# Which engine waits for the last store: GpSimd in place of SyncE at the end of a batched matmul

## The chip, the cores and the metric

One core of one Trainium2 chip. The metric is the device time of one execution in microseconds (us), median of several runs. The kernel before takes 125.6 us.

## The reference

```python
batch, m, k, n = 16, 512, 512, 512          # a: [16, 512, 512], b: [16, 512, 512], float32
def reference(a, b):
    return np.matmul(a, b.transpose(0, 2, 1)).astype(np.float32)
```

## The kernel before

The kernel loads `a` and `b` in 16 transfers of 2 MB, casts to bf16, transposes and multiplies on TensorE, evicts on ScalarE, and stores 16 results of 1 MB. Semaphores are handled by hand inside two critical sections. GpSimd (POOL in the profile) issues the stores 0 to 7, SyncE (SP) the stores 8 to 15, and each store has its own semaphore `s_st[n]`.

```python
    with tc.tile_critical(no_gpsimd_drain=True):
        # ... buffers, semaphores, loads ...
        STORES = "SSSSOSOSOSSOOOOOO"        # GpSimd: S issues a store, O hands a buffer back
        LATE = {11: (8, 9), 13: (10, 11), 15: (12, 13)}     # SyncE's stores, by load

        def landed(n):
            return s_st[n], 16

        def store(n):
            engine = nc.gpsimd if n < STORES.count("S") else nc.sync
            engine.wait_ge(s_out, n + 1)
            engine.dma_start(
                out[n].rearrange("(p j) n -> p j n", j=J), ob[:, n % NO]
            ).then_inc(s_st[n], 16)
        # ... SyncE: loads and its stores, then:
        store(batch - 2)
        store(batch - 1)
        for n in range(batch - NO, batch - 1):
            nc.sync.wait_ge(*landed(n))
        # ... VectorE, ScalarE, TensorE ...

    with tc.tile_critical(no_gpsimd_drain=True):
        nc.sync.wait_ge(*landed(batch - 1))
```

Leaving a section is a handshake: the engine that heads the section gives a signal, the other engines of the section answer, each with a drain (with `no_gpsimd_drain`, GpSimd with a plain NOP). After the second section the program closes by itself: every engine drains, GpSimd gathers their signals and releases them, clears the semaphores, and does this barrier once more. GpSimd's own drain stands just ahead of its gathering.

## Time and profile before

| | before |
|---|---|
| time, median | 125.6 us |
| span, first to last instruction | 123.9 us |
| the last store lands | 122.52 us |
| from there to the end of the span | 1.41 us |
| GpSimd's first closing DRAIN | 120.40 to 121.11 us, 714 ns |

The times of single instructions below are read from the trace, to the nanosecond. "Landing" is the 16th and last increment of the last store's semaphore. The quoted views give starts to 0.1 us. In them a row such as `L287 POOLq DRAIN  x3: 34/130/714, 123.3 to 124.7; - x3` names the source line, the engine (q: handled by its sequencer), the operation, how many there were, the shortest, median and longest duration in ns, and the start of the first and the last. L287 is the end of the program, to which the closing barrier is booked; L260 is the `with` of the second section.

### The profile page before, as it was taken

How to read it: one execution, taken by the hardware profiler on the slowest of the kernel's cores; microseconds unless marked ns; L12 is line 12 of the kernel's file. 1: busy time of each engine (PE TensorE's matmuls, PEld its weight loads, DVE VectorE, ACT ScalarE, POOL GpSimd, SP SyncE). 2: the span in 40 equal slices, each digit the busy share in tenths (PEclk: the TensorE clock that was granted, in tenths of full speed). 3: DMA queues.
4: the chain of work that ended last, by engine and by line, in shares of the span. 5: the costliest groups of instructions: out<-in, count | busy, mean ns of one | idle time of the engine just before them, and what ended most of it. 6: DMA issues, size and time to landing. Idle time of an engine off the chain costs nothing. (4 is left out here: it accounts for less than half of the span.)

```text
span 123.9 us, 2364 instructions
## 1 busy us (share of the span) xinstructions
PE 91.9 (74%) x768; PEld 56.9 (46%) x768; DVE 68.5 (55%) x96; ACT 68.0 (55%) x130; POOL 5.5 (4%) x14
## 2 busy tenths in 40 slices
PE   0005099998999899999989998996699919995000
PEld 0005096457447644764575467444554518441000
DVE  0006596938891897489478658914957068400000
ACT  4002415669558937876595579534956069655000
POOL 2000000000000070001010120000000000000000
PEclk9999999999999999999999999999999986999955
DMA  4999999999999998999999999999999999999980
GB/s 95 397 423 434 428 428 428 423 434 423 428 434 439 439 423 360 439 439 412 436 420 431 450 420 420 431 431 450 410 436 428 410 434 423 423 431 426 434 368 8
DMA packets 4608, 50.33 MB, mean 406 GB/s; under 512 B 512, under 2 KB 512, under 8 KB 512
## 3 DMA queue, kind: packets, MB, share of 16 engines
q1 hardware_dynamic: 3456, 41.94, 80.3%
q0 software_dynamic: 1152, 8.39, 16.0%
HBM read 33.55 MB, written 16.78 MB: 406 GB/s over the span
## 5 line engine op out<-in xcount | busy, mean ns | idle before, releaser
L247 PE MATMUL ps<-tb,ta 128*128 128x512 bf16 x256 | 57.8, 379 | 0.5
L205 ACT COPY ob<-ps 128x512 f32 x64 | 34.4, 589 | 31.1 <-PE ps L247 21.5
L187 ACT COPY ta<-tp 128x512 bf16<-128x512 bf16 x64 | 32.8, 610 | 13.8 <-PE tp L228 13.8
L247 PEld LDWEIGHTS ps<-tb,ta 128*128 128x128 bf16 x256 | 24.1, 97 | 30.6 <-issue 4.0
L228 PE MATMUL tp<-ident,ha 128*128 128x128 bf16 x256 | 20.1, 234 | 14.1 <-PEq L133 14.1
L228 PEld LDWEIGHTS tp<-ident,ha 128*128 128x128 bf16 x256 | 17.0, 105 | 17.9 <-issue 16.0
L168 DVE COPY tb<-tp 128x1024 bf16<-128x1024 bf16 x32 | 21.2, 684 | 4.8 <-DVEq L133 4.8
L228 PE MATMUL tp<-ident,hb 128*128 128x128 bf16 x256 | 18.8, 232 | 6.7 <-PEq L133 6.7
L228 PEld LDWEIGHTS tp<-ident,hb 128*128 128x128 bf16 x256 | 16.6, 105 | 7.2 <-issue 7.2
L152 DVE CAST hb<-ld 128x1024 bf16 x8 | 5.5, 689 | 12.6 <-DVEq L133 12.5
L163 DVE COPY ha<-wa 128x2048 bf16<-128x2048 bf16 x8 | 5.5, 690 | 11.1 <-DVEq L133 11.1
L152 DVE CAST ha<-ld 128x1024 bf16 x8 | 5.6, 705 | 9.8 <-DVEq L133 9.8
L158 DVE CAST wa<-ld 128x2048 bf16 x8 | 9.8, 1220 | 0.0
L158 DVE CAST wb<-ld 128x2048 bf16 x8 | 9.8, 1219 | 0.0
L103 POOL DMA_DIRECT2D out_dram<-ob x8 | 4.8, 607 | 65.5 <-DMA ld<-in_b_dram 41.5
L155 DVE CAST ha<-ld 128x1024 bf16 x8 | 5.6, 700 | 0.0
L167 DVE COPY hb<-wb 128x2048 bf16<-128x2048 bf16 x8 | 5.5, 685 | 0.2
L155 DVE CAST hb<-ld 128x1024 bf16 x8 | 5.5, 686 | 0.0
L178 ACT ACT_TABLE_LOAD x1 | 1.3, 1283 | 1.1 <-SPq L43 1.1
L79 POOL TENSOR_SCALAR_AFFINE_SELECT ident<-ident 128x128 bf16<-128x128 bf16 x1 | 0.3, 284 | 0.2 <-POOL ident L77 0.2
L77 POOL MEMSET ident<- 128x128 bf16 x1 | 0.2, 205 | 0.5 <-SPq L43 0.5
L178 ACT COPY one<-const-float32-1.0 128x1 f32<-128x1 f32 x1 | 0.2, 192 | 0.0
(4 smaller groups left out, 0.4 us busy)
## 6 DMA issues: line engine op xcount, KB each, us to landing
ld<-in_a_dram SPq DMA_DIRECT2D x8, 2048.0 KB, 28.1
ld<-in_b_dram SPq DMA_DIRECT2D x8, 2048.0 KB, 30.4
out_dram<-ob POOLq DMA_DIRECT2D x8, 1024.0 KB, 29.2
out_dram<-ob SPq DMA_DIRECT2D x8, 1024.0 KB, 19.7
```

The costliest lines, as they stand in the source:

```text
L103: engine.dma_start(out[n].rearrange("(p j) n -> p j n", j=J), ob[:, n % NO]).then_inc(s_st[n], 16)
L152: nc.vector.tensor_copy(out=h[:, :J, :], in_=src[:, :J, :HK]).then_inc(s_cd, 1)
L155: nc.vector.tensor_copy(out=h[:, J:, :], in_=src[:, J:, :HK]).then_inc(s_c, 1)
L158: nc.vector.tensor_copy(out=w[:], in_=src[:, :, HK:]).then_inc(s_w, 1)
L163: nc.vector.tensor_copy(out=ha[:], in_=wa[:]).then_inc(s_ca, 1)
L167: nc.vector.tensor_copy(out=hb[:], in_=wb[:]).then_inc(s_cb, 1)
L168: nc.vector.tensor_copy(out=tb[:, ko, :], in_=tp[:, 2 + ko % 2].rearrange("k j p -> k (j p)"),).then_inc(s_eb, 1)
L178: nc.scalar.copy(out=one[:], in_=nc.const_aps.tensor(1.0, (P, 1), f32))
L187: c = nc.scalar.copy(out=ta[:, ko, e * J * P:(e + 1) * J * P].rearrange("k (j p h) -> k j p h", j=J, h=2), in_=tp[:, ko % 2, :, e * HP:(e ...
L205: c = nc.scalar.copy(out=dst[:, j, :].rearrange("m (p j) -> m p j", j=2 * J), in_=ps[:, j, :].rearrange("m (j p) -> m p j", j=2 * J),)
L228: t = nc.tensor.transpose(tp[:, 2 * x + g, j, :], h[:, j, g * P:(g + 1) * P], ident[:])
L247: t = nc.tensor.matmul(ps[:, j, :], ta[:, ko, (e * J + j) * P:(e * J + j + 1) * P], tb[:, ko, :].rearrange("k (j p) -> k j p", j=2 * J)[:, ...
```

## The change

The wait for the last store, the only instruction of the second section, goes to another engine. The intent is to take the last wait off SyncE.

```diff
     with tc.tile_critical(no_gpsimd_drain=True):
-        nc.sync.wait_ge(*landed(batch - 1))
+        nc.gpsimd.wait_ge(*landed(batch - 1))
```

## The prediction

> **What bounds the kernel now.** The kernel before takes 125.58 us (125.56 to 125.77); its profiled execution took 125.75 us, of which the span from first to last instruction is 123.9 us. I call the remaining 1.85 us launch overhead and take it as unchanged, because no instruction of the kernel lies in it. I read the whole page first, to see what is full:
>
> ```profile
> PE   0005099998999899999989998996699919995000
> POOL 2000000000000070001010120000000000000000
> DMA  4999999999999998999999999999999999999980
> DMA packets 4608, 50.33 MB, mean 406 GB/s; under 512 B 512, under 2 KB 512, under 8 KB 512
> ```
>
> The DMA row stands at 9 from the second slice to the last but two: the 50.33 MB of loads and stores set the time, and the matrix engine stops three slices (some 9 us) before the end. GpSimd (POOL) is nearly empty. The change touches no load, store or computation, so the body of the kernel, up to the last store, should be the same to the noise. All that can move is the tail, so I then read windows of the end (columns: window, length, busy us of each engine with instruction counts, granted clock, DMA share, GB/s):
>
> ```profile
> core 0: us, PE busy (x) PEld busy (x) DVE busy (x) ACT busy (x) POOL busy (x), PEclk, DMA share, GB/s
> ...
> 118.00:120.00 2.00, 0.00 (x0) 0.00 (x0) 0.00 (x0) 0.00 (x0) 0.00 (x0) 0.58 1.00 422
> 120.00:121.00 1.00, 0.00 (x0) 0.00 (x0) 0.00 (x0) 0.00 (x0) 0.00 (x0) 0.50 0.49 205
> 121.00:122.50 1.50, 0.00 (x0) 0.00 (x0) 0.00 (x0) 0.00 (x0) 0.00 (x0) 0.50 0.04 16
> 122.50:123.90 1.40, 0.00 (x0) 0.00 (x0) 0.00 (x0) 0.00 (x0) 0.00 (x0) 0.50 0.00 0
> ```
>
> Data moves at full rate until 120, trickles until 122.5, and then there are 1.4 us without data or computation. The last store is issued at 113.95 and takes 8.6 us to land (the view of DMA issues), so it lands at 122.52. The wait for it is the last line here (SyncE's own waits; total us, times, longest):
>
> ```profile
> SPq L119 <- DMA out_dram<-ob: 5.7, 3, 2.4
> ...
> SPq L287 <- DMA out_dram<-ob: 1.7, 1, 1.7
> ```
>
> L119 is the three earlier waits for stores inside the first section, L287 (the line that closes the program) the one that the change moves. The sequencer instructions of L287, by engine:
>
> ```profile
> L287 SPq EVENT_SEMAPHORE  x5: 17/28/1689, 120.7 to 123.9; - x5
> L287 POOLq EVENT_SEMAPHORE  x4: 17/17/17, 123.0 to 123.8; - x4
> L287 POOLq DRAIN  x3: 34/129/714, 120.4 to 123.7; - x3
> L287 SPq DRAIN  x3: 7/7/7, 122.9 to 123.2; - x3
> ...
> L287 POOLq EVENT_SEMAPHORE_RANGE_CLEAR  x1: 287/287/287, 123.4 to 123.4; - x1
> ```
>
> (duration ns min/median/max, start of the first and the last.) The 1689 ns is SyncE waiting for the last store, 120.86 to 122.55. The 714 ns is GpSimd's own first DRAIN of the closing barrier, started at 120.40 and done at 121.11: at present it is finished 1.4 us before the last store lands, so it is free. That is the fact on which my prediction rests.
>
> **What the Trainium skill says.** Perfetto Trace Analysis, section Sequencer-only Instruction: the reported time of such an instruction is its execution alone, not its semaphore wait. The single waits here agree (GpSimd's gathering wait shows 17 ns although GpSimd stood there for 1.9 us); the two-semaphore wait for the last store differs, it shows the whole 1689 ns. PSUM — Partial Sum Buffer, section Engine vs sequencer instructions: a drain waits for the engine to go fully idle. Here SyncE, ScalarE and VectorE drain in 7 to 10 ns and GpSimd in 34 to 714 ns, the longest one 15 us after GpSimd's previous instruction, so idleness alone doesn't explain its cost. GPSIMD Engine Reference, section Instruction dispatch: a GpSimd instruction passes its sequencer and then a dispatcher on eight cores; I take this as a possible reason for a dear drain, which no number here proves. DMA: Bandwidth & Descriptors, section Why a DMA increments its semaphore by 16 and not by 1: only the full 16 means landed. The trace agrees: the last store's 15th increment comes at 121.28, the 16th at 122.52. Which engine waits doesn't move that.
>
> **The change, part by part.** Removed: SyncE's wait for the last store, and with it SyncE's part in the second section. Added: the same wait on GpSimd, preceded on GpSimd by the entry waits of the section, which on SyncE are two of 28 ns plus gaps, over by 120.86. They stay under the 1.7 us for which the store is still in flight: cost nothing.
> Moved: what follows the landing. Before, by the starts in the trace: landing 122.524; SyncE's wait ends 122.546; its branch 122.584 (33 ns); the leaving handshake of the section 122.739, 122.824 and 122.897; two SyncE drains 122.941 and 123.005; GpSimd's gathering wait 123.036. That is 0.51 us from landing to gather. From the gather to the end (release, drain 129 ns, clearing of the semaphores 287 ns, drain 34 ns, second barrier) it is 0.90 us, the same in both kernels.
> After: GpSimd sees the landing (22 ns), branches (38 ns gap and 33 ns), answers the section's handshake (122 ns gap, as SyncE had after its branch, and 13 ns for its NOP as at the end of the first section), and 65 ns later starts its drain: some 0.30 us. The drain is now behind the landing in GpSimd's program order. If it costs again 0.714 us, GpSimd reaches the gather at 0.30 + 0.71 + 0.03 = 1.04 us after landing. SyncE's leg (hears GpSimd's answer, its NOP and two drains, some 0.13 us after it) is over at about 0.4 us and doesn't count. Difference: 1.04 - 0.51 = +0.53 us. In general the difference is the drain's exposed length minus 0.18 us.
> I don't trust the 714 ns fully: the drain before ran beside saturated DMA (205 GB/s on average in that microsecond), the later one will run in quiet, and other GpSimd drains took 34 and 129 ns (188 ns at the start, with four memsets just ahead). I expect 0.4 to 0.7 us and take 0.6 us: 0.6 - 0.18 = +0.42 us, so 125.58 + 0.42 = 126.0 us.
>
> **The rivals.**
> First, the drain is cheap when DMA is quiet (129 ns as in the second one): -0.05 us, 125.5 us. For it: three of the four GpSimd drains were short. Against: those three each had GpSimd work or another drain just before, while the long one came after a long pause, and the new one also will.
> Second, GpSimd's route is shorter than SyncE's and the tail improves: SyncE spends 0.49 us from landing to its signal, mostly gaps between tiny instructions; GpSimd must only answer once before its own drain. With a 34 ns drain the SyncE leg would end at some 0.40 us, giving -0.1 us, 125.5 us. Against: the drain is not optional, and a 34 ns one appears only right after another.
> Third, GpSimd wakes late from a semaphore wait, or the wait disturbs its stores. Against: GpSimd passed the first section's end 23 ns after the signal like the others (20 to 28 ns), and its last store was issued at 71.4, so nothing of it is left to delay. It would add under 0.3 us: 126.3 us.
> Fourth, the body shifts because SyncE's issue order changes. Nothing in the first section changes, so I give it nothing beyond the spread of 0.2 us between runs.
>
> **Range and chances.** The terms leave -0.1 to +0.6 us, and the spread of the runs adds 0.1 to 0.2: 125.4 to 126.4 us. Two per cent is 2.5 us, more than the whole 1.4 us after the landing, so only a disturbed run could cross it: faster 0.01, same 0.98, slower 0.01.
>
> **What would show it right or wrong.** Right: no SyncE wait for the last store at the close, a long wait on GpSimd instead; GpSimd's first closing DRAIN starting about 0.3 us after the landing and lasting 0.4 to 0.7 us; 1.6 to 2.0 us from landing to the end where it was 1.41; the DMA row unchanged. Wrong: that drain under 0.2 us, or still ahead of the landing (then the section's exit would be ordered otherwise than I think), or a difference that lies before the last landing.

## The result, and the profile after

The changed kernel takes 126.31 us (126.04 to 126.72, six runs), the kernel before 125.6 us (six runs). The ratio is 1.0054, with a 95% interval of 1.0032 to 1.0076: same, by the 2% measure, and slower by some 0.7 us.

The page's rows of the changed kernel, for the body (40 slices of the span, busy share in tenths, and the packets moved):

```profile
PE   0005099998999899899989998994799827993000
POOL 2000000000000190010020400000000000000000
DMA  5899999999999999999999999999999999999950
DMA packets 4608, 50.33 MB, mean 403 GB/s; under 512 B 512, under 2 KB 512, under 8 KB 512
```

The body is as before: the same packets and bytes, and DMA at 8 or 9 tenths in every slice but the first and the last two. The mean rate fell from 406 to 403 GB/s because the span is longer. The windows at the end (window, length, busy us of each engine, granted clock, DMA share, GB/s):

```profile
118.00:120.00 2.00, 0.00 (x0) 0.00 (x0) 0.00 (x0) 0.00 (x0) 0.00 (x0) 0.57 0.98 414
120.00:121.00 1.00, 0.00 (x0) 0.00 (x0) 0.00 (x0) 0.00 (x0) 0.00 (x0) 0.50 0.32 131
121.00:122.70 1.70, 0.00 (x0) 0.00 (x0) 0.00 (x0) 0.00 (x0) 0.00 (x0) 0.50 0.05 19
122.70:124.90 2.20, 0.00 (x0) 0.00 (x0) 0.00 (x0) 0.00 (x0) 0.00 (x0) 0.50 0.00 0
```

The stretch without data at the end is now 2.2 us long where it was 1.4. SyncE's own waits in the tail (total us, times, longest):

```profile
SPq L119 <- DMA out_dram<-ob: 5.7, 3, 2.4
SPq L287 <- POOLq L260: 2.3, 1, 2.3
```

The waits for the earlier stores, at the end of the first section (L119), are unchanged. At the close SyncE waits no more for a transfer but for GpSimd's signal from the second section. GpSimd's instructions of the closing line:

```profile
L287 POOLq EVENT_SEMAPHORE  x7: 17/17/1664, 121.0 to 124.8; - x7
L287 POOLq DRAIN  x3: 34/130/714, 123.3 to 124.7; - x3
L287 POOLq COMPARE_BRANCH  x2: 33/33/33, 0.8 to 122.9; - x2
L287 POOLq EVENT_SEMAPHORE_RANGE_CLEAR  x1: 287/287/287, 124.3 to 124.3; - x1
```

The 1664 ns are GpSimd's wait for the last store. The three drains last 34, 130 and 714 ns as before (34, 129, 714), but the first now starts at 123.3 in place of 120.4, behind the landing. From the trace, in us after the landing:

| | before | after |
|---|---|---|
| landing, us from the span's start | 122.524 | 122.797 |
| branch out of the section | SyncE 0.060 | GpSimd 0.074 |
| GpSimd's 714 ns DRAIN starts | -2.125 | 0.460 |
| SyncE's last DRAIN of the first closing barrier | 0.481 | 0.463 |
| GpSimd gathers | 0.512 | 1.218 |
| end of the span | 1.412 | 2.119 |

The difference of the tails, 2.119 - 1.412 = 0.71 us, arises between the landing and the gather; from the gather to the end it is 0.90 us in both. The landing itself came 0.27 us later in this trace and 0.07 us later in a second trace of the same kernel, so it varies by itself from run to run. The spans of the two traces therefore differ by 0.98 us, 0.27 of it ahead of the landing.

### The profile page after: what moved, and what is told of

The parts are those of the page before. It is cut to its first block, busy times and chain, and to the rows that moved or that the text cites. A ratio compares the mean times of both kernels' runs of the same rounds, so it can differ in the third digit from the quotient of the medians.

```text
span 124.9 us, 2365 instructions
## 1 busy us (share of the span) xinstructions
PE 90.6 (72%) x768; PEld 55.6 (45%) x768; DVE 68.2 (55%) x96; ACT 68.1 (55%) x130; POOL 6.7 (5%) x14
## 3 DMA queue, kind: packets, MB, share of 16 engines
q0 software_dynamic: 1152, 8.39, 15.9%
## 5 line engine op out<-in xcount | busy, mean ns | idle before, releaser
L228 PE MATMUL tp<-ident,ha 128*128 128x128 bf16 x256 | 19.3, 230 | 14.6 <-PEq L133 14.6
L228 PEld LDWEIGHTS tp<-ident,ha 128*128 128x128 bf16 x256 | 16.5, 103 | 18.1 <-issue 16.3
L228 PE MATMUL tp<-ident,hb 128*128 128x128 bf16 x256 | 17.8, 225 | 7.7 <-PEq L133 7.4
L228 PEld LDWEIGHTS tp<-ident,hb 128*128 128x128 bf16 x256 | 15.7, 101 | 8.5 <-issue 8.5
L103 POOL DMA_DIRECT2D out_dram<-ob x8 | 6.0, 758 | 64.0 <-DMA ld<-in_b_dram 41.7
```

The costliest lines, as they stand in the source:

```text
L103: engine.dma_start(out[n].rearrange("(p j) n -> p j n", j=J), ob[:, n % NO]).then_inc(s_st[n], 16)
L228: t = nc.tensor.transpose(tp[:, 2 * x + g, j, :], h[:, j, g * P:(g + 1) * P], ident[:])
```

## The experiments

Theory A: GpSimd's closing drain is dear, and the change puts it behind the landing. Rival C: the drain matters little, the wait is dear on any engine other than SyncE, because the section is then headed by another engine with a longer handshake. Within A: why is one drain 714 ns and another 34? Twelve kernels were run, one of them the changed kernel unaltered; each edit is against the changed kernel.

**after_again: the changed kernel unaltered**, beside the next three on the same chip.

> The changed kernel unaltered, on the same chip as the next three, as their yardstick. Both theories: 1.0054 of the kernel before (126.2 to 126.4 us), 2.12 us from the last store's landing to the end of the span against 1.41 us before, with GpSimd's first closing DRAIN at 714 ns.

Measured: 126.44 us, ratio 1.0050 (1.0032 to 1.0069), landing to end 2.119 us, drain 714 ns. The tail repeats to the nanosecond or one off, and so does the ratio within its interval.

**drain_before_wait: an early drain.**

```diff
+        nc.gpsimd.drain()
         nc.gpsimd.wait_ge(*landed(batch - 1))
```

> One explicit GpSimd drain put ahead of the wait for the last store, in the shadow of the store. Theory A (the first drain after GpSimd's stores is dear, later ones are cheap): the explicit drain shows some 714 ns before the landing, the closing DRAIN after it 34 to 190 ns, landing to end falls from 2.12 to about 1.53 us, the time is 0.1 to 0.2 us over the kernel before (ratio 1.001). Theory B (a drain behind the wait is dear by itself, whatever came before): closing DRAIN 714 ns again, 2.12 us, ratio 1.0054.

Measured: 125.67 us, ratio 0.9992 (0.9972 to 1.0012). GpSimd's drains, the explicit one at L261, those of the closing line now at L288:

```profile
L261 POOLq DRAIN  x1: 714/714/714, 121.1 to 121.1; - x1
L288 POOLq DRAIN  x3: 34/34/130, 123.0 to 123.7; - x3
```

The 714 ns went to the explicit drain, which lies in the shadow of the store, and the closing one takes 34 ns. Landing to end is 1.389 us. Theory B is out: a drain isn't dear for standing behind the wait. The tail came out shorter than the 1.53 us of theory A's expectation, because the drain shrank to 34 ns (I had put 130) and because the wait is now carried by the branch itself, so that the drain starts 0.41 us after the landing in place of 0.46.

**act_waits: ScalarE waits.**

```diff
-        nc.gpsimd.wait_ge(*landed(batch - 1))
+        nc.scalar.wait_ge(*landed(batch - 1))
```

> ScalarE in place of GpSimd waits for the last store in the second section; it heads the section as GpSimd does in the changed kernel. Theory A (the exposed GpSimd drain is the cost): GpSimd's drain is hidden ahead of the landing again, landing to end 1.40 to 1.60 us, ratio 0.999 to 1.002. Rival C (taking the wait off SyncE is the cost, through the longer handshake between two engines): landing to end about 2.0 us or more, ratio 1.004 to 1.006.

Measured: 125.66 us, ratio 0.9990 (0.9975 to 1.0006), landing to end 1.388 us.

```profile
L287 POOLq DRAIN  x3: 34/130/714, 120.3 to 123.6; - x3
```

The first drain starts at 120.3 again, ahead of the landing, and the loss is gone, though the wait is off SyncE (the tail is 0.01 us below the range that theory A gave). Rival C falls: it isn't the leaving of SyncE that costs, it is where GpSimd's drain stands.

**sp_heads_section: SyncE runs the handshake, GpSimd waits.**

```diff
-    with tc.tile_critical(no_gpsimd_drain=True):
+    with tc.tile_critical(sync_engine=nc.sync.engine, no_gpsimd_drain=True):
         nc.gpsimd.wait_ge(*landed(batch - 1))
```

> GpSimd still waits, but SyncE is named as the engine that opens and closes the second section, so that GpSimd answers one handshake and doesn't run it. Theory A with my handshake term as predicted: landing to the start of GpSimd's DRAIN 0.30 us in place of 0.46 us, the DRAIN 714 ns, landing to end about 1.95 us, ratio 1.004. Rival C (the handshake is the larger part): landing to end under 1.6 us, ratio under 1.002.

Measured: 126.19 us, ratio 1.0030 (1.0013 to 1.0048). The drain, 714 ns (`L287 POOLq DRAIN  x3: 34/129/714, 122.8 to 124.2; - x3`), starts 0.314 us after the landing in place of 0.460, and landing to end is 1.971 us in place of 2.119. So heading the section, in place of only answering, costs 0.15 us of the 0.71. Rival C, for which the handshake would be the larger part, falls here too. The intervals of 1.0030 and 1.0050 overlap; the trace separates the two, the times alone don't.

**drain_after_wait: the suspected cost doubled.**

```diff
         nc.gpsimd.wait_ge(*landed(batch - 1))
+        nc.gpsimd.drain()
```

> The suspected cost doubled: a second GpSimd drain behind the wait for the last store, ahead of the closing one. If only the first drain after the stores is dear, the explicit one shows 714 ns and the closing one some 34 ns, and landing to end rises from 2.12 us by 0.08 to 0.15 us. If every drain behind a wait is dear, both show 714 ns and landing to end is about 2.9 us, some 1.5 us over the kernel before (ratio 1.012).

Measured: 126.08 us, ratio 1.0039 (1.0014 to 1.0063).

```profile
L262 POOLq DRAIN  x1: 714/714/714, 122.3 to 122.3; - x1
L288 POOLq DRAIN  x3: 34/34/130, 123.3 to 124.0; - x3
```

Only the first of the two behind the landing is dear, as theory A has it. One number of the expectation failed: landing to end should have risen by 0.08 to 0.15 us and fell to 1.985 us. The explicit drain carries the wait itself and starts 0.025 us after the landing, and the branch that stood behind the landing in the changed kernel now stands ahead of it.

**memset_before_wait: GpSimd's cores at work shortly before.**

```diff
+        nc.gpsimd.memset(wake[:], 0.0)          # wake: one column of its own
         nc.gpsimd.wait_ge(*landed(batch - 1))
```

> A memset of one column on GpSimd ahead of the wait for the last store, so that GpSimd's cores have worked some 1.6 us before the closing DRAIN. Pause theory (a long pause since GpSimd's last work makes the drain dear): the DRAIN behind the landing falls to 34 to 190 ns and landing to end to about 1.5 us. Stores theory (the stores that GpSimd issued since its last drain make it dear): the DRAIN stays at 714 ns, landing to end 2.1 us.

Measured (a single look): the memset, 98 ns long, started 1.38 us ahead of the landing, the drain took 714 ns, landing to end 2.070 us.

```profile
L289 POOLq DRAIN  x3: 34/130/714, 122.9 to 124.3; - x3
```

The pause theory falls.

**pool_stores_0, pool_stores_1, pool_stores_4: fewer stores on GpSimd.** The rest go to SyncE's list; for four:

```diff
-    STORES = "SSSSOSOSOSSOOOOOO"
-    LATE = {11: (8, 9), 13: (10, 11), 15: (12, 13)}
+    STORES = "SSSSOOOOOOOOO"
+    LATE = {7: (4, 5), 9: (6, 7), 11: (8, 9), 13: (10, 11), 15: (12, 13)}
```

> The changed kernel with all eight of GpSimd's stores issued by SyncE; the body's timing may shift, only the closing DRAIN is read. Stores theory: the DRAIN behind the landing shows 34 to 190 ns and landing to end is about 1.4 to 1.55 us. Pause theory: 714 ns still, since GpSimd has done nothing for over 100 us, and 2.12 us.

> The changed kernel with one store on GpSimd and seven moved to SyncE. Stores theory, in proportion to their number: the DRAIN behind the landing takes about 34 + 680/8 = 120 ns. Stores theory, once for any number: 714 ns. Pause theory: 714 ns.

> The changed kernel with four stores on GpSimd and four moved to SyncE. The closing DRAIN behind the landing took 41 ns with none, 135 ns with one and 714 ns with eight. A drain that grows with the number of stores: 135 + 3 x 83 = about 380 ns, landing to end about 1.78 us. A drain that saturates early or jumps: near 135 or near 714 ns.

Measured: the closing drains of the three kernels, with no, one and four stores on GpSimd, in this order. The one behind the landing is the first to start:

```profile
L287 POOLq DRAIN  x3: 34/41/117, 125.2 to 126.0; - x3
```

```profile
L287 POOLq DRAIN  x3: 34/117/135, 124.5 to 125.3; - x3
```

```profile
L287 POOLq DRAIN  x3: 34/130/387, 123.9 to 124.9; - x3
```

By the order in the trace it takes 41, 135 and 387 ns, against 714 ns with eight stores; landing to end is 1.433, 1.527, 1.792 and 2.119 us. From none to eight that is (714 - 41)/8 = 84 ns a store. The stores theory holds: the drain is some 40 ns plus a part in proportion to their number. In these single looks, whose state is unknown, the kernels took longer (128.04, 127.40 and 127.01 us), and the last store landed at 124.8, 124.1 and 123.4 us. That wasn't taken further; the looks give no sign that taking stores off GpSimd to save its drain is a gain here.

**pool_stores_4_halved and pool_stores_4_by_rows: bytes, rows or transfers?** Four stores on GpSimd, each issued as two transfers, cut once along the row and once by partition:

```diff
-            engine.dma_start(rows, ob[:, n % NO])
+            for h in range(2):      # halved: all 128 partitions, 4 KB of each row
+                engine.dma_start(rows[:, 2*h:2*h+2], ob[:, n % NO, 2*h:2*h+2])
+            for h in range(2):      # by rows: 64 partitions, whole rows of 8 KB
+                engine.dma_start(rows[HP*h:HP*h+HP], ob[HP*h:HP*h+HP, n % NO])
```

(One loop in each kernel; the semaphore of such a store then counts to 32.)

> The same four stores on GpSimd, each issued as two transfers of 512 KB: the bytes of four stores, the count of eight. If the drain counts transfers: about 714 ns. If it goes by bytes: about 380 ns.

> The same four stores on GpSimd, each issued as two transfers of 64 partitions with whole 8 KB rows: the count of eight transfers, but each with half the rows (64 in place of 128), so the rows of four stores in all. Halving the row length left the drain at 714 ns. If the drain counts transfers: about 714 ns again. If it counts rows: about 387 ns.

Measured: 714 ns in both:

```profile
L292 POOLq DRAIN  x3: 34/130/714, 126.3 to 127.7; - x3
```

```profile
L292 POOLq DRAIN  x3: 34/130/714, 123.3 to 124.7; - x3
```

Eight transfers of half the bytes, whether with as many rows as eight whole stores or with half as many, drain like eight whole stores. The drain counts transfers. Nor does it go by packets: GpSimd's queue (q0 in the view of DMA) carried 1152 in the changed kernel, 576 with four whole stores, 1152 halved and 640 by rows.

**one_section: SyncE waits, but without the second section.**

```diff
-        for n in range(batch - NO, batch - 1):
+        for n in range(batch - NO, batch):
             nc.sync.wait_ge(*landed(n))
 ...
-    with tc.tile_critical(no_gpsimd_drain=True):
-        nc.gpsimd.wait_ge(*landed(batch - 1))
```

> No second section: SyncE waits for the last store at the end of the first, so the first section's exit and GpSimd's first DRAIN come behind the landing although SyncE waits. Theory A: GpSimd passes the exit 0.28 us after the landing, drains from 0.36 us for 714 ns, landing to end about 2.0 us, ratio 1.004 to 1.005. If the engine that waits were the cause: about 1.4 us, ratio 1.000.

Measured: 126.29 us, ratio 1.0035 (1.0013 to 1.0056), landing to end 2.013 us; the ratio is a little under the expected 1.004 to 1.005, which lies within its interval.

```profile
L285 POOLq DRAIN  x3: 34/129/714, 122.8 to 124.2; - x3
```

SyncE waits, and the loss is there all the same: GpSimd can leave the first section only after the landing, and its drain starts 0.356 us after it. This is the counterpart of act_waits, and it shows what the second section does for the kernel before: GpSimd, free of it, drains while the last store is on its way.

No version beat the kernel before: drain_before_wait and act_waits have a tail 0.02 us shorter (1.389 and 1.388 against 1.412 us), and both intervals include 1.

## Why the prediction was right or wrong

The range (125.4 to 126.4 us) holds the measured 126.31 us, and the class was right. The mechanism was right too, but the sizes were not: the terms alone ended at +0.6 us, the tail measured +0.71, and only the allowance for the spread of the runs kept the time inside. Of the signs named beforehand the order of things came true, and the three sizes were each overshot: the drain's start (0.46 for about 0.3 us), its length (714 ns for 0.4 to 0.7 us), and landing to end (2.12 for 1.6 to 2.0 us). Point by point:

- **The body doesn't move.** Right as far as the runs show: same packets, same bytes. Of the two traces' difference 0.71 us lies behind the landing; the 0.27 us ahead of it shrink to 0.07 in the second trace of the same kernel.
- **The entry waits on GpSimd are hidden.** Right: they end at 121.16 us, 1.6 us before the landing.
- **The drain comes behind the landing.** Right, and it is the cause, shown from both sides: put it ahead (drain_before_wait, act_waits) and the loss goes; put it behind by other means (one_section) and it returns.
- **The drain's length.** I took 0.6 us, because I thought that 714 ns was partly due to the busy DMA beside it. It was 714 ns again, to the nanosecond. This term was undersized by 0.11 us. The distrust rested on a misread window: the 205 GB/s are the mean of 120 to 121 us, and most of it moved before the drain began at 120.40. Cut at the drain, the windows (below this list) show DMA at a share of 0.12 and 46 GB/s beside it. So the drain ran beside a nearly idle DMA already in the kernel before, and whether a full DMA would lengthen it was not tested by any run.
- **0.30 us from the landing to the drain.** It was 0.46 us. I had given GpSimd one answer to a handshake that SyncE runs. In fact GpSimd, as the only engine in the section, heads it: it signals, answers itself and waits for its own answer. With SyncE as the head it was 0.314 us, so the step was costed well for a handshake that doesn't take place. This is the larger miss, 0.16 us.
- **The sum.** With the two terms as measured it is 0.46 + 0.714 + 0.04 = 1.22 us to the gather, against 0.51 before: +0.71 us, where I had +0.42.
- **The first rival, a cheap drain in quiet,** was rightly set back, but for a wrong reason. I held that the three short drains were short because GpSimd had worked just before, and the long one long because of the pause. The memset just ahead left it at 714 ns, and a pause of over 100 us without stores gave 41 ns. My "15 us after GpSimd's previous instruction" passed over the NOP of the section's exit, which ended 65 ns before the drain. What counts is the number of transfers that GpSimd has issued since its last drain, some 84 ns each. With none since, drains took 34 to 130 ns behind the landing; why the second closing one takes 117 to 130 and the third 34 wasn't looked into.
- **The second rival, a shorter route over GpSimd,** needs a cheap drain: with 34 ns (drain_before_wait) the tail does get 0.02 us shorter. But there the branch carries the wait, which saves 0.05 us. On the changed kernel's own route, with a drain of 41 ns (pool_stores_0), GpSimd gathers 0.545 us after the landing, against 0.512 with SyncE waiting. So the route alone is worth some 0.03 us either way; the undrained stores are what costs.
- **The third rival, a GpSimd that wakes late or is hurt by its stores.** GpSimd wakes hardly later: its branch comes 0.074 us after the landing, 0.014 us more than on SyncE. "Nothing of it is left to delay" was true of the stores, which had all landed by 105 us, and not of what they leave behind for the drain.

The kernel before, ahead of the drain and during it (columns as in the windows above):

```profile
119.00:120.40 1.40, 0.00 (x0) 0.00 (x0) 0.00 (x0) 0.00 (x0) 0.00 (x0) 0.50 0.98 415
120.40:121.11 0.71, 0.00 (x0) 0.00 (x0) 0.00 (x0) 0.00 (x0) 0.00 (x0) 0.50 0.12 46
```

The PSUM — Partial Sum Buffer page (section Engine vs sequencer instructions), which the prediction used, says that a drain waits for the engine to be idle. The last of GpSimd's stores had landed 18 us before the drain that took 714 ns, so waiting for a store on its way isn't what takes the time. Whether GpSimd still had something else to do, and what it does in 84 ns for each transfer, stays open; the runs show the count, not the mechanism.

## What to carry to other kernels

In this kernel a GpSimd drain cost some 84 ns for each transfer that GpSimd had issued since its last one, even 18 us after they had landed. Where you see the same, see to it that the drain, an explicit one if need be, runs while something else is still on its way. Look at the last transfer's landing and list what each engine must still do after it: a wait moved from one engine to another moves everything that stands behind the wait in that engine's program. A cost that was hidden before showed in the trace with its full duration, 714 ns, and came out at that duration when it was exposed; before you discount such a figure for what ran beside it, cut a window exactly at the instruction and look.

## What the Trainium skill lacked or had wrong

- No page gives the cost of a drain on GpSimd after transfers issued there. Lacking in GPSIMD Engine Reference and in DMA: Bandwidth & Descriptors: 41, 135, 387 and 714 ns after 0, 1, 4 and 8 transfers, 714 ns for eight transfers of half the bytes, 34 to 130 ns with no transfer since the last drain.
- PSUM — Partial Sum Buffer, section Engine vs sequencer instructions, says a drain "waits for the engine to go fully idle". It doesn't say what that can take when nothing is seen to run: on GpSimd 714 ns, 18 us after the last of its stores had landed. The runs don't show whether GpSimd was idle in the page's sense.
- Perfetto Trace Analysis, section Sequencer-only Instruction, says that the profile reports the execution and not the semaphore wait. That holds for the single waits seen here (the drain of drain_after_wait starts 0.025 us after the landing and shows 714 ns). An instruction that waits for two semaphores shows its wait in some cases: 1689 ns before and 1664 after, where the trace names the last store's semaphore second. In the L119 rows of the kernel before, where the late semaphore is named first, waits of up to 2.4 us show as 28 ns, as the page says (`L119 SPq EVENT_SEMAPHORE  x3: 17/28/28, 115.1 to 120.1; - x3`).
